# Up projection with the tokens' high and low parts as one 512-column moving operand

## The chip, the cores and the metric

One core of a Trainium2 chip runs the whole layer. The time is that of one execution on the device in microseconds; three runs of the kernel before have a median of 1557.48 us.

## The reference, cut to what matters

One layer of a transformer over 256 tokens of width 2048: an attention block, and then a gated MLP whose up projection is what changes here. All inputs and the output are float32.

```python
z = modulate(rms_norm(x, norm2_g), sh2, sc2)      # 256 x 2048
u = z @ w_up                                      # 256 x 11264 (2 * D_FF, D_FF = 5632)
up = jnp.pad(u, ((0, 0), (1, 1), (0, 0)))
uc = conv_b + sum(conv_w[j] * up[:, j:j + 256] for j in range(3))   # along the tokens
a, b = jnp.split(uc, 2, axis=-1)
x = x + g2 * ((jax.nn.silu(a) * b) @ w_down)
out = rms_norm(x, final_norm_g)
```

## The kernel before

**Three products for one.** A float32 product is made of products of float32r halves. `hi_lo` (line 182) splits a tensor: ScalarE copies it into float32r (`hi`), VectorE subtracts that copy (`lo`). `mm3` then adds three products into a PSUM bank: hi·hi, hi·lo and lo·hi. The first operand is the stationary one (128 x 128), the second the moving one. The tokens' parts in the MLP are `z2h` and `z2l` (tiles sZL and sX in the trace), made by `z2_parts` beside the first products.

**Up projection.** The 11264 columns are 88 tiles of 128. `up_group` (line 1271) takes eight such tiles, and of the last columns of each half four: the weights are stationary, all 256 tokens move, and each tile's result is half of a 512-column PSUM bank. For each of 16 tiles of the contraction (`kt`) a unit of weights (128 x 1024) is multiplied: 8 tiles x 3 products of 256 columns, 24 matmuls. A group fills four of the eight banks; the next group fills the other four while the first is evacuated.

**Weights.** SyncE loads 1 MB (two units) into a ring of four `raw` buffers. Each unit is split into `hi` (ScalarE, CAST) and `lo` (VectorE, TENSOR_TENSOR), of which there are three buffers each: the CAST of a unit waits until TensorE has finished the unit three earlier. `take` keeps two units split ahead of the one in use.

**Evacuation.** `conv` (line 1253) reads the bank: for each tile an ACTIVATE on ScalarE (bias and middle tap), then two SCALAR_TENSOR_TENSOR on VectorE. A group of the first half then gets Silu on ScalarE, one of the second half is multiplied into it on VectorE.

**Order.** TensorE issues in program order. ScalarE and VectorE run in the order in which the scheduler put their instructions. A pacing object lets lanes, the evacuation among them, go a step further when little work is left to VectorE and ScalarE by its estimate. One lane, `rest`, does not belong to the MLP: it forms the gate `g2` out of `w_ada` on VectorE (SCALAR_TENSOR_TENSOR acc<-raw, 128 x 1024) beside the first groups, through the same `raw` ring.

**Down projection.** It follows at once (512-column matmuls, eight banks, the tokens' parts stationary).

Of the kernel before, what the change touches and what calls it, by code (L numbers as in the profile page):

```python
# [10 lines left out]
F32R = mybir.dt.float32r  # L11
# [5 lines left out]
P = 128  # L17
D = 2048
KT = D // P
T = 256  # L20
# [30 lines left out]
class Pace:  # L51
    """Order of emission. TensorE issues in the order emitted; beside the big products run lanes, generators
    that are taken a step further when enough TensorE work lies behind their last step and when VectorE and
    ScalarE have little left to do. A step yields the TensorE time (us) that the next one should stay behind."""
# [51 lines left out]
    def finish(self, *gens):  # L106
        # what is left of these lanes, a step of each in turn
        gens = list(gens)
        self.lanes = [x for x in self.lanes if not any(x[0] is g for g in gens)]
        while gens:  # L110
            gens = [g for g in gens if next(g, None) is not None]
# [7 lines left out]
class Engine:  # L119
    """An engine whose instructions are counted into the pace."""  # L120
# [30 lines left out]
def _build(tc, nc, es, a):  # L151
# [30 lines left out]
    def hi_lo(hi, lo, src):  # L182
        # src = hi + lo exactly: float32r holds the upper half of the significand in hi, the rest in lo
        ACT.copy(hi, src)
        DVE.tensor_sub(lo, src, hi.bitcast(F32))

    def split(src, shape):
        h = units.tile(shape, F32R, tag="hi", name="hi")
        l = units.tile(shape, F32R, tag="lo", name="lo")
        hi_lo(h, l, src)  # L190
        return h, l

    # the weights of the big products, in program order: loaded and split ahead of the products that take them
# [49 lines left out]
    # x and ctx tokens, raw  # L243
# [9 lines left out]
    # conditioning, contraction index k = p * 16 + j  # L253
# [11 lines left out]
    # per-column vectors, turned to one value a partition  # L265
# [25 lines left out]
    def lane_tables():  # L291
        # the other vectors, and the rope tables with the gains of the normalised heads folded in
        r = slot("X0", [P, 4, P])
        POOL.memset(r, 0.0)
        nc.sync.dma_start(r[0:88, 0, :], a["conv_b"][0].rearrange("(r c) -> r c", c=P))
        nc.sync.dma_start(r[96:100, 0, :], a["mla_kv_norm_g"][0].rearrange("(r c) -> r c", c=P))
        nc.sync.dma_start(r[100:106, 0, :], a["mla_q_norm_g"][0].rearrange("(r c) -> r c", c=P))
        for j in range(3):
            nc.sync.dma_start(r[0:88, 1 + j, :], a["conv_w"][0, j].rearrange("(r c) -> r c", c=P))
        nc.sync.dma_start(tabB, a["ropeB"].rearrange("w (t p) d -> p w t d", p=P))  # L300
        nc.sync.dma_start(tabA, a["ropeA"].rearrange("w (t p) d -> p w t d", p=P))
        nc.sync.dma_start(gqk[:, 0, :], a["gqa_q_norm_g"].partition_broadcast(P)[:, 0, :])
        nc.sync.dma_start(gqk[:, 1, :], a["gqa_k_norm_g"].partition_broadcast(P)[:, 0, :])
        yield 25.0
        turn_vectors(1, 4, flat(r))
        yield 0.0
        for w in range(2):
            g = gqk[:, w, :]
            gv = g.rearrange("p (x h q) -> p x h q", x=2, h=2)
            for t in range(2):  # L310
                DVE.tensor_mul(tabG[:, w, 0, t, :], tabB[:, 0, t, :], g)
                o = tabG[:, w, 1, t, :].rearrange("p (x h q) -> p x h q", x=2, h=2)
                s = tabB[:, 1, t, :].rearrange("p (x h q) -> p x h q", x=2, h=2)
                for h in range(2):
                    DVE.tensor_mul(o[:, :, h, :], s[:, :, h, :], gv[:, :, 1 - h, :])
                yield 0.0

# [63 lines left out]
    def gemv_chunk(ci):  # L381
        # first shift and scale of both conditionings, the columns that part ci of the contraction needs
# [111 lines left out]
    # how many of its loads it may take: a result's slot has to be free when it comes to it  # L494
# [24 lines left out]
    def group_T(ps, w, mov, first, last):  # L519
        wh, wl = w  # L520
        mh, ml = mov
        for n in range(wh.shape[1] // P):
            mm3(ps[n // 2][:, (n % 2) * T:(n % 2 + 1) * T], wh[:, n * P:(n + 1) * P], wl[:, n * P:(n + 1) * P],
                mh, ml, first and n % 2 == 0, last)

# [87 lines left out]
    # the same blocks' weights  # L613
    def rows2(w, nk, c0, cn, kt0=0):
        # one k tile a unit, two a load
        for k0, kn in halves(nk):
            r = load(w[(kt0 + k0) * P:(kt0 + k0 + kn) * P, c0:c0 + cn].rearrange("(k p) c -> p k c", p=P), [P, kn, cn])
            for k in range(kn):
                yield split(r[:, k, :], [P, cn])

    def weights():
# [30 lines left out]
        for g in range(6):  # L652
            for half in range(2):
                yield from rows2(a["w_up"][0], KT, half * FF + g * 1024, min(8, FT - 8 * g) * P)
# [5 lines left out]

    stream = weights()
# [57 lines left out]
    def rope(dst, src, cc, ssn, heads, q, tA, tB):  # L719
        # dst = src * cc + swap(src) * ssn, heads of 4 * q columns  # L720
# [89 lines left out]
    def attn_head(passes, scale, v, oh, ol, ptag):  # L810
        # one head: scores of both query tiles, softmax over all keys, P V
# [147 lines left out]
    # branch B's attention beside the last part of the input projection  # L959
# [258 lines left out]
    z2h = [slot(f"ZL{i}", [P, 8, T], F32R) for i in range(2)]  # L1218
    z2l = [slot(f"X{2 + i}", [P, 8, T], F32R) for i in range(2)]

    def z2_parts():
        for n in range(4):
# [5 lines left out]
            for j in range(0, 4, 2):  # L1228
# [4 lines left out]
                for k in range(2):  # L1233
# [3 lines left out]
                    hv, lv = z2h[kt // 8][:, kt % 8, :], z2l[kt // 8][:, kt % 8, :]  # L1237
# [15 lines left out]
    def conv(dst, ps, col, turns):  # L1253
        # two tiles of columns, their steps in turn or one after the other
# [16 lines left out]
    def up_group(g, half, zgen=None):  # L1271
        nt = min(8, FT - 8 * g)
        if half == 0:
            hid.append(slot(hslots[g], [P, nt, T]))
        hs = hid[g]
        c0 = half * FF + g * 1024
        ps = [bank() for _ in range(nt // 2)]
        for kt in range(KT):
            w = take()
            if zgen is not None and kt % 2 == 0:  # L1280
                next(zgen, None)
            group_T(ps, w, (z2h[kt // 8][:, kt % 8, :], z2l[kt // 8][:, kt % 8, :]), kt == 0, kt == KT - 1)
            yield

        def end():
            for n2 in range(nt // 2):
                hv = flat(hs[:, 2 * n2:2 * n2 + 2, :])
                d = hv if half == 0 else scratch([P, 512])
                conv(d, ps[n2], c0 // P + 2 * n2, (g, half) == (5, 1))
# [24 lines left out]
    for g in range(6):  # L1314
        for half in range(2):
            run(up_group(g, half, zgen if g + half == 0 else None))
# [6 lines left out]
    w_d = a["w_down"][0]  # L1323
    ps = [[bank() for _ in range(4)] for _ in range(2)]
# [18 lines left out]
    # the last part bank by bank, so that the end of one runs beside the products of the next  # L1343
# [47 lines left out]
def _rope_tables(rot):  # L1391
    # cos and signed sin of the grid positions, laid out as (axis, half, frequency) columns
# [29 lines left out]
```

## Time and profile before

| | |
|---|---|
| three runs | 1556.18, 1557.48, 1559.08 us |
| profiled execution, span | 1556.9 us |
| TensorE busy | 1514.9 us, 97% |
| VectorE busy | 1079.2 us, 69% |
| ScalarE busy | 747.3 us, 48% |
| up projection, first product to last | about 791 to 1307 us |
| down projection | from about 1307 us |

Times in the trace count from the span's start. An engine's busy time is what its instructions took; overlapping ones count once. PEld is TensorE's weight load, which runs beside the products. DMA share is the mean busy share of the core's 16 DMA engines. The profiled execution's span lies 0.6 us under the median of the runs.

### The profile page before, as it was taken

How to read it: one execution, taken by the hardware profiler on the slowest of the kernel's cores; microseconds unless marked ns; L12 is line 12 of the kernel's file. 1: busy time of each engine (PE TensorE's matmuls, PEld its weight loads, DVE VectorE, ACT ScalarE, POOL GpSimd, SP SyncE). 2: the span in 40 equal slices, each digit the busy share in tenths (PEclk: the TensorE clock that was granted, in tenths of full speed). 3: DMA queues.
4: the chain of work that ended last, by engine and by line, in shares of the span. 5: the costliest groups of instructions: out<-in, count | busy, mean ns of one | idle time of the engine just before them, and what ended most of it. 6: DMA issues, size and time to landing. Idle time of an engine off the chain costs nothing.

```text
span 1556.9 us, 25677 instructions
## 1 busy us (share of the span) xinstructions
PE 1514.9 (97%) x10641; PEld 1387.7 (89%) x10641; DVE 1079.2 (69%) x1489; ACT 747.3 (48%) x1081; POOL 14.3 (1%) x23
## 2 busy tenths in 40 slices
PE   6999999999999999999989999999999999999997
PEld 5777888899998988997879999999999999888886
DVE  3457686798778888697878787656546566555556
ACT  4634242355775446543346445454444545444454
POOL 0000000010000000000000000000000000000000
PEclk9999999999999999999989999999999999999999
DMA  9778788755346885478967877555555447555552
GB/s 359 240 252 321 276 323 286 259 180 190 109 143 201 288 279 187 160 265 307 350 217 249 318 278 273 182 182 173 187 190 185 162 141 245 189 192 195 199 197 81
DMA packets 105380, 350.59 MB, mean 225 GB/s; under 512 B 6846, under 2 KB 20392, under 8 KB 98736
## 3 DMA queue, kind: packets, MB, share of 16 engines
q1 hardware_dynamic: 105264, 348.96, 64.8%
q8 instruction: 83, 1.36, 0.3%
q14 instruction: 33, 0.27, 0.1%
HBM read 346.84 MB, written 2.10 MB: 224 GB/s over the span
## 4 chain that ended last, share of the span: by engine, by line
PE 90%; DMA 5%; DVE 3%; ACT 1%; issue 1%; SPq 0%; ACTq 0%; POOLq 0%; POOL 0%; DVEq 0%
PE bank L210 86%; DMA raw<-in_w_ada 2%; PE bank L219 2%; PE bank L398 2%; DMA raw<-in_w_in 1%; DVE lo L140 1%; DVE acc L140 1%; DMA raw<-in_w_out 1%; DVE sK L140 1%; DMA sK<-in_x 0%; DVE sX L140 0%; DVE scratch L140 0%; ACT hi L140 0%; ACT scratch L140 0%; DVE sG L140 0%
## 5 line engine op out<-in xcount | busy, mean ns | idle before, releaser
L140 DVE TENSOR_TENSOR lo<-raw,hi 128x1024 fp32r<-128x1024 f32 (+3 forms) x479 | 551.6, 1154 | 336.5 <-ACT hi L140 333.3
L140 ACT CAST hi<-raw 128x1024 fp32r<-128x1024 f32 (+3 forms) x479 | 474.6, 993 | 624.3 <-PE bank L210 512.9
L210 PE MATMUL bank<-sZL,hi 128*128 128x256 f32 (+1 forms) x3168 | 740.9, 285 | 2.5 <-ACT hi L140 2.5
L210 PE MATMUL bank<-sZL,lo 128*128 128x256 f32 x2352 | 667.5, 284 | 0.6 <-DVE lo L140 0.6
L210 PEld LDWEIGHTS bank<-sZL,hi 128*128 128x128 f32 (+1 forms) x3168 | 551.4, 192 | 14.5 <-issue 7.5
L210 PEld LDWEIGHTS bank<-sZL,lo 128*128 128x128 f32 x2352 | 452.2, 192 | 1.1 <-DVE lo L140 1.1
L210 PE MATMUL bank<-sX,hi 128*128 128x256 f32 x1536 | 435.6, 284 | 0.5 <-DVE sX L140 0.5
L210 PEld LDWEIGHTS bank<-sX,hi 128*128 128x128 f32 x1536 | 295.8, 193 | 1.3 <-DVE sX L140 0.8
L210 PE MATMUL bank<-hi,sZC 128*128 128x512 f32 (+1 forms) x816 | 261.1, 383 | 0.0
L210 PEld LDWEIGHTS bank<-hi,sZC 128*128 128x128 f32 x816 | 152.5, 188 | 30.0 <-issue 0.3
L140 DVE SCALAR_TENSOR_TENSOR acc<-raw,cs,acc 128x1024 f32<-128x1024 f32 x120 | 153.6, 1280 | 14.2 <-DMA raw<-in_w_ada 13.2
L210 PE MATMUL bank<-lo,sZC 128*128 128x512 f32 (+1 forms) x344 | 131.4, 382 | 0.0
L210 PEld LDWEIGHTS bank<-lo,sZC 128*128 128x128 f32 x344 | 64.7, 188 | 12.8 <-DVE lo L140 0.3
L140 DVE TENSOR_TENSOR sK<-bank,sK 128x512 f32<-128x512 f32 (+1 forms) x92 | 59.9, 685 | 10.1 <-PE bank L210 8.8
L210 PE MATMUL bank<-hi,sZL 128*128 128x512 f32 x192 | 63.3, 392 | 0.0
L210 PE MATMUL bank<-lo,sX 128*128 128x512 f32 x128 | 50.1, 391 | 1.9 <-DVE lo L140 1.9
L210 PE MATMUL bank<-sZC,hi 128*128 128x256 f32 x256 | 50.4, 284 | 1.4 <-DVE sZC L140 1.4
L210 PE MATMUL bank<-hi,sX 128*128 128x512 f32 x128 | 50.4, 394 | 0.1
L140 DVE TENSOR_TENSOR sG<-bank,sG 128x512 f32<-128x512 f32 x64 | 41.9, 683 | 5.9 <-PE bank L210 5.8
L210 PEld LDWEIGHTS bank<-hi,sZL 128*128 128x128 f32 x192 | 36.1, 188 | 9.4 <-issue 1.5
L398 PE MATMUL bank<-raw,cs 128*32 128x512 f32 (+2 forms) x320 | 37.7, 514 | 5.1 <-DMA raw<-in_w_ada 4.9
L210 PEld LDWEIGHTS bank<-sZC,hi 128*128 128x128 f32 x256 | 39.0, 184 | 2.5 <-DVE sZC L140 1.6
(195 smaller groups left out, 1266.7 us busy)
## 6 DMA issues: line engine op xcount, KB each, us to landing
raw<-in_w_ada SPq DMA_DIRECT2D x82, 1024.0 KB, 5.7
raw<-in_w_up SPq DMA_DIRECT2D x80, 1024.0 KB, 5.1
raw<-in_w_down SPq DMA_DIRECT2D x44, 1024.0 KB, 4.9
raw<-in_w_in SPq DMA_DIRECT2D x37, 1024.0 KB, 7.6
raw<-in_w_out SPq DMA_DIRECT2D x16, 1024.0 KB, 8.3
raw<-in_w_ada SPq DMA_DIRECT2D x16, 768.0 KB, 6.1
raw<-in_w_br_b SPq DMA_DIRECT2D x8, 1024.0 KB
raw<-in_w_br_a SPq DMA_DIRECT2D x8, 1024.0 KB, 6.7
```

Of the source, the lines that this page charges most:

```text
L140: return f(*args, **kw)
L210: PE.matmul(out, lhsT, rhs, start=start, stop=stop, skip_group_check=True)
L219: PE.transpose(out, src, ident[:n, :n])
L398: PE.matmul(ps[32 * g:32 * g + 32, :cols], cs[:, j0 + jj, :], w[:, jj, :], start=j0 + j == 0, stop=j0 + j == 14, skip_group_check=True)
```

## The change

The first group (8 tiles, `up_first`) keeps the old products, since the tokens' parts are only then being made. The other 80 tiles go in 20 parts of four (`up_part`). Tile and bank are now one to one: a single matmul multiplies the weights' hi with hi and lo of the tokens side by side (2 x 256 columns), so that hi·hi lies in the first half of the bank and hi·lo in the second, and a second matmul of 256 columns adds lo·hi to the second half. At the end `halves_sum` copies the first half to SBUF and adds the second to it; `conv` reads that sum. A unit of weights is now 2 contraction tiles x 512 columns, and a load 4 x 512 columns: as many bytes as before, in rows of 2 KB instead of 4 KB.

```diff
-    z2h = [slot(f"ZL{i}", [P, 8, T], F32R) for i in range(2)]
-    z2l = [slot(f"X{2 + i}", [P, 8, T], F32R) for i in range(2)]
+    z2 = [slot(x, [P, 2, 4, T], F32R) for x in ("ZL0", "ZL1", "X2", "X3")]
...
+    def group_W(ps, wh, wl, mov, first, last):
+        for n, p in enumerate(ps):
+            c = slice(n * P, (n + 1) * P)
+            mm(p.rearrange("p (s t) -> p s t", s=2), wh[:, c], mov, first, False)
+            mm(p[:, T:2 * T], wl[:, c], mov[:, 0, :], False, last)
+
+    def halves_sum(ps):
+        u = scratch([P, 512])
+        for i in range(2):
+            ACT.copy(u[:, i * T:(i + 1) * T], ps[i][:, 0:T])
+        for i in range(2):
+            d = u[:, i * T:(i + 1) * T]
+            DVE.tensor_add(d, ps[i][:, T:2 * T], d)
+        return u
...
+    def rows4(w, nk, c0):
+        for k0 in range(0, nk, 4):
+            r = load(w[k0 * P:(k0 + 4) * P, c0:c0 + 512].rearrange("(k p) c -> p k c", p=P), [P, 4, 512])
+            for u in range(2):
+                yield split(r[:, 2 * u:2 * u + 2, :], [P, 2, 512])
...
-        for g in range(6):
-            for half in range(2):
-                yield from rows2(a["w_up"][0], KT, half * FF + g * 1024, min(8, FT - 8 * g) * P)
+        yield from rows2(a["w_up"][0], KT, 0, 1024)
+        for c0 in up_cols[1:]:
+            yield from rows4(a["w_up"][0], KT, c0)
...
+    def up_part(g, half, sub):
+        hs = hid[g]
+        c0 = (half * FF + g * 1024 + sub * 512) // P
+        ps = [bank() for _ in range(4)]
+        for k2 in range(0, KT, 2):
+            wh, wl = take()
+            for k in range(2):
+                kt = k2 + k
+                group_W(ps, wh[:, k, :], wl[:, k, :], z2[kt // 4][:, :, kt % 4, :], kt == 0, kt == KT - 1)
+                yield
+
+        def end():
+            us = []
+            for n2 in range(2):
+                us.append(halves_sum(ps[2 * n2:2 * n2 + 2]))
+                yield 0.0
+            for n2 in range(2):
+                hv = flat(hs[:, 4 * sub + 2 * n2:4 * sub + 2 * n2 + 2, :])
+                d = hv if half == 0 else scratch([P, 512])
+                conv(d, us[n2], c0 + 2 * n2, (g, half) == (5, 1))
...
-    ps = [[bank() for _ in range(4)] for _ in range(2)]
+    ps = [[None] * 4 for _ in range(2)]
+    for n2 in range(0, 4, 2):
+        for t in range(2):
+            for n in range(n2, n2 + 2):
+                ps[t][n] = bank()
```

On TensorE, inside a group of the up projection, two tiles before (sZL is the tokens' hi, sX their lo; hi and lo without a prefix are the weights'):

```order
L210 MATMUL bank<-sZL_8144,hi 128x256
L210 MATMUL bank<-sX_8146,hi 128x256
L210 MATMUL bank<-sZL_8144,lo 128x256
L210 MATMUL bank<-sZL_8144,hi 128x256
L210 MATMUL bank<-sX_8146,hi 128x256
L210 MATMUL bank<-sZL_8144,lo 128x256
```

and the end of the first group and the first three tiles of a part now (one tile, sZL_8144, holds hi and lo):

```order
L210 MATMUL bank<-sX_8147,hi 128x256 x2
L210 MATMUL bank<-sX_8147,lo 128x256
L210 MATMUL bank<-sZL_8144,hi 128x512
L210 MATMUL bank<-sZL_8144,lo 128x256
L210 MATMUL bank<-sZL_8144,hi 128x512
L210 MATMUL bank<-sZL_8144,lo 128x256
L210 MATMUL bank<-sZL_8144,hi 128x512
```

Three matmuls for a tile have become two, with as many columns in all.

On VectorE, where a group of the first half ends late in the up projection (sX is the group's result), before:

```order
L140 TENSOR_TENSOR lo<-raw,hi 128x1024 x11
L140 SCALAR_TENSOR_TENSOR sX_12348<-bank,vec,sX_12348 128x255 x4
L140 TENSOR_TENSOR lo<-raw,hi 128x1024
L140 SCALAR_TENSOR_TENSOR sX_12348<-bank,vec,sX_12348 128x255 x4
L140 TENSOR_TENSOR lo<-raw,hi 128x1024
```

and where a part with the same columns ends now (scratch is the sum's buffer):

```order
L140 TENSOR_TENSOR lo<-raw,hi 128x1024 x5
L140 TENSOR_TENSOR scratch<-bank,scratch 128x256 x3
L140 TENSOR_TENSOR lo<-raw,hi 128x1024
L140 TENSOR_TENSOR scratch<-bank,scratch 128x256
L140 SCALAR_TENSOR_TENSOR sX_11626<-scratch,vec,sX_11626 128x255 x8
L140 TENSOR_TENSOR lo<-raw,hi 128x1024 x7
```

The splits were interleaved with four steps of the convolution at a time; now four adds and eight such steps stand round a single split.

On ScalarE at the same place now:

```order
L140 COPY scratch<-bank 128x256 x3
L140 CAST hi<-raw 128x1024
L140 COPY scratch<-bank 128x256
L140 ACTIVATE sX_11626<-scratch,vec 128x256 x4
L140 CAST hi<-raw 128x1024
L140 ACTIVATE sX_11626<-sX_11626 128x512
L140 CAST hi<-raw 128x1024
```

The four COPY are new; the second CAST stands behind four ACTIVATE that each wait for an add.

## Rows read from the trace of the kernel before

**Rows 1.** The page: span, TensorE, and the chain that ended last.

```profile
span 1556.9 us, 25677 instructions
...
PE 1514.9 (97%) x10641; PEld 1387.7 (89%) x10641; DVE 1079.2 (69%) x1489; ACT 747.3 (48%) x1081; POOL 14.3 (1%) x23
...
PE 90%; DMA 5%; DVE 3%; ACT 1%; issue 1%; SPq 0%; ACTq 0%; POOLq 0%; POOL 0%; DVEq 0%
```

**Rows 2.** Stretches: PE, PEld, DVE, ACT, POOL busy (records); clock, DMA share, GB/s.

```profile
890.50:936.60 46.10, 46.10 (x387) 46.10 (x386) 40.09 (x48) 21.42 (x27) 0.00 (x0) 1.00 0.80 292
1000.00:1290.00 290.00, 290.00 (x2419) 290.00 (x2419) 172.14 (x227) 138.43 (x176) 0.00 (x0) 1.00 0.53 174
1265.00:1300.00 35.00, 35.00 (x294) 35.00 (x293) 24.86 (x44) 18.99 (x33) 0.00 (x0) 1.00 0.66 197
1320.00:1500.00 180.00, 180.00 (x796) 149.10 (x795) 94.72 (x100) 79.97 (x100) 0.00 (x0) 1.00 0.57 194
```

**Rows 3.** Groups by form, 830 to 1290 us: busy, mean ns | idle before.

```profile
L210 PE MATMUL bank<-sZL,hi 128*128 128x256 f32 x1268 | 359.7, 284 | 0.0
...
L140 DVE TENSOR_TENSOR lo<-raw,hi 128x1024 fp32r<-128x1024 f32 x147 | 179.9, 1224 | 138.8 <-ACT hi L140 137.0
L140 ACT CAST hi<-raw 128x1024 fp32r<-128x1024 f32 x146 | 152.9, 1047 | 209.4 <-PE bank L210 203.2 <-issue 4.5 <-ACT scratch L140 0.9
L140 DVE SCALAR_TENSOR_TENSOR scratch<-bank,vec,scratch 128x255 f32<-128x255 f32 x80 | 35.0, 477 | 0.4
L140 DVE SCALAR_TENSOR_TENSOR acc<-raw,cs,acc 128x1024 f32<-128x1024 f32 x26 | 33.3, 1281 | 3.8 <-DMA raw<-in_w_ada 3.6
...
L140 ACT ACTIVATE scratch<-bank,vec 128x256 f32<-128x256 f32 x40 | 21.5, 564 | 7.3 <-DVE scratch L140 5.7 <-PE bank L210 1.3
...
L140 DVE TENSOR_TENSOR sG<-sG,scratch 128x512 f32<-128x512 f32 x16 | 11.0, 688 | 0.1
```

**Rows 4.** TensorE timeline where lengths mix (attention's value products): start us, us.

```profile
561.53 0.28 PE L210 MATMUL bank<-hi,sK 128*128 128x256 f32 x1
561.65 0.63 PE L210 MATMUL bank<-sK,hi 128*128 128x512 f32 x2
...
562.81 0.39 PE L210 MATMUL bank<-sK,lo 128*128 128x512 f32 x1
563.04 0.28 PE L210 MATMUL bank<-hi,sK 128*128 128x256 f32 x1
563.15 0.28 PE L210 MATMUL bank<-lo,sK 128*128 128x256 f32 x1
```

**Rows 5.** Groups by form, whole run: the nearest to the new operations.

```profile
L140 ACT ACTIVATE sZC<-sX,md 128x256 fp32r<-128x256 f32 x16 | 8.7, 591 | 1.1 <-DVE sX L140 1.1
...
L140 DVE TENSOR_TENSOR sX<-bank,sZL 128x256 fp32r<-128x256 f32 x8 | 3.4, 419 | 0.9 <-ACT sZL L140 0.9
...
L140 ACT COPY sY<-bank 128x256 f32<-128x256 f32 x8 | 2.9, 365 | 1.5 <-PE bank L210 1.5
```

**Rows 6.** VectorE timeline at a group's end: start us, us.

```profile
983.78 1.65 DVE L140 SCALAR_TENSOR_TENSOR scratch<-bank,vec,scratch 128x255 f32<-128x255 f32 x4
985.52 1.23 DVE L140 TENSOR_TENSOR lo<-raw,hi 128x1024 fp32r<-128x1024 f32 x1
986.66 1.65 DVE L140 SCALAR_TENSOR_TENSOR scratch<-bank,vec,scratch 128x255 f32<-128x255 f32 x4
```

**Rows 7.** ScalarE timeline inside a group, with what ended its wait.

```profile
1021.88 1.05 ACT L140 CAST hi<-raw 128x1024 fp32r<-128x1024 f32 x1 [1.83 <-PE bank L210]
```

**Rows 8.** VectorE timeline, the same unit's lo.

```profile
1022.95 1.23 DVE L140 TENSOR_TENSOR lo<-raw,hi 128x1024 fp32r<-128x1024 f32 x1 [1.66 <-ACT hi L140]
```

**Rows 9.** TensorE timeline, first units of the down projection.

```profile
1311.47 0.74 PE L210 MATMUL bank<-hi,sZC 128*128 128x512 f32 x2
...
1313.12 0.40 PE L210 MATMUL bank<-hi,sZC 128*128 128x512 f32 x1
```

**Rows 10.** Waits: ScalarE's for the loads of the up weights, 770 to 1300 us.

```profile
ACT hi L140 <- DMA raw<-in_w_up: 3.1, 1, 3.1
```

More of the change, by code (lines that the diff above doesn't have):

```diff
@@ L659, in weights @@
                 yield (hx, *split(r[:, u * 1024:(u + 1) * 1024], [P, 1024]))
+    up_parts = [(0, 0, None)]
+    for g in range(6):
+        for half in range(2):
+            for sub in range(min(8, FT - 8 * g) // 4):
+                if g + half > 0:
+                    up_parts.append((g, half, sub))
+    up_cols = [0] + [half * FF + g * 1024 + sub * 512 for g, half, sub in up_parts[1:]]
     stream = weights()
@@ L1236, in z2_parts @@
                     pv = ps[:, k * T:(k + 1) * T]
-                    hv, lv = z2h[kt // 8][:, kt % 8, :], z2l[kt // 8][:, kt % 8, :]
+                    hv, lv = z2[kt // 4][:, 0, kt % 4, :], z2[kt // 4][:, 1, kt % 4, :]
                     ACT.activation(hv, pv, AF.Identity, bias=s2col[:, kt:kt + 1], scale=a2col[:, kt:kt + 1])
@@ L1269, in h_split, with up_first @@
         return hx
[L1271 to L1277, printed above, removed]
+    def up_first(zgen):
+        ps = [bank() for _ in range(4)]
         for kt in range(KT):
             w = take()
-            if zgen is not None and kt % 2 == 0:
+            if kt % 2 == 0:
                 next(zgen, None)
-            group_T(ps, w, (z2h[kt // 8][:, kt % 8, :], z2l[kt // 8][:, kt % 8, :]), kt == 0, kt == KT - 1)
+            group_T(ps, w, (z2[kt // 4][:, 0, kt % 4, :], z2[kt // 4][:, 1, kt % 4, :]), kt == 0, kt == KT - 1)
             yield
         def end():
-            for n2 in range(nt // 2):
-                hv = flat(hs[:, 2 * n2:2 * n2 + 2, :])
+            for n2 in range(4):
+                hv = flat(hid[0][:, 2 * n2:2 * n2 + 2, :])
+                conv(hv, ps[n2], 2 * n2, False)
+                yield 0.0
+                ACT.activation(hv, hv, AF.Silu)
+                yield 0.0
+        evacs["up"] = pace.add(end(), limit=LIM_EVAC, prio=0)
+    def up_part(g, half, sub):
+        hs = hid[g]
+        c0 = (half * FF + g * 1024 + sub * 512) // P
+        ps = [bank() for _ in range(4)]
+        for k2 in range(0, KT, 2):
[8 more added lines that the diff above has]
+                us.append(halves_sum(ps[2 * n2:2 * n2 + 2]))
+                yield 0.0
+            for n2 in range(2):
+                hv = flat(hs[:, 4 * sub + 2 * n2:4 * sub + 2 * n2 + 2, :])
                 d = hv if half == 0 else scratch([P, 512])
-                conv(d, ps[n2], c0 // P + 2 * n2, (g, half) == (5, 1))
+                conv(d, us[n2], c0 + 2 * n2, (g, half) == (5, 1))
                 yield 0.0
@@ L1313, in _build @@
     pace.add(rest, after=20.0, limit=REST_LIM_U, dma=REST_DMA, prio=9)
-    for g in range(6):
-        for half in range(2):
-            run(up_group(g, half, zgen if g + half == 0 else None))
+    for g, half, sub in up_parts:
+        if half == 0 and not sub:
+            hid.append(slot(hslots[g], [P, min(8, FT - 8 * g), T]))
+        run(up_first(zgen) if sub is None else up_part(g, half, sub))
     finish(evacs["up"])
```

## The prediction

> **What bounds the kernel now.** I read the page first: TensorE is busy for 97% of the span, and the chain that ended last is 90% TensorE [rows 1]. So the question is what TensorE does in the up projection and whether anything makes it wait there. The groups of 830 to 1290 us give each of the three kinds of products no idle time before it [rows 3], and the stretch of 1000 to 1290 us has TensorE and its weight load busy throughout at the full granted clock of 1.00, the 2.4 GHz level, while VectorE is busy for 59% and ScalarE for 48% [rows 2]. TensorE's stream alone sets the time here; the rest has room. Busy time of overlapping matmuls says nothing of the price of one, so I take start-to-start times from counts: 2419 records less some three that reach over the edges in 290 us are 0.120 us for a matmul of 256 columns, and 796 less two in 180 us of the down projection are 0.227 us for one of 512 [rows 2]. At 2.4 GHz the columns alone would take 0.1067 and 0.2133 us: both lengths carry the same 13 to 14 ns on top. That is what the change works on.
>
> **What it removes.** For one tile and one contraction tile, three matmuls of 256 columns (0.360 us) become one of 512 and one of 256 (0.347 us). Where the lengths mix today, 256 columns are followed by the next matmul after 0.12 us and 512 columns after 0.23 us [rows 4], so I add the two prices. Saved: 13 ns, 80 tiles x 16 times, 1280 x 0.013 = **16.6 us**. The first group, 8 tiles, keeps its price. The clock is not at stake: it is 1.00 in all these stretches [rows 2], and TensorE remains without pauses if the rest of this working holds.
>
> Here a rule speaks against the size of it. The page "TensorE: Matmul & The Clock Gate" of the Trainium skill (section "Wait — 56ns, not 53.3ns?") gives a warm matmul a fixed cost of about 2.5 ns over its columns. By that the saving would be 1280 x 2.5 ns = 3.2 us, an estimate from that page. The trace does not agree: 13.3 ns over 256 columns and 13.7 over 512.
>
> **What it adds.** Each of the 80 tiles gets a COPY on ScalarE and an add on VectorE. The nearest rows are a COPY of 128 x 256 from a bank, 365 ns, and an add of 128 x 256 with a bank as one input, 419 ns [rows 5]. The convolution now reads SBUF: its ACTIVATE costs 591 ns [rows 5] for 564 [rows 3]; its SCALAR_TENSOR_TENSOR I leave at 477. In all 33.5 us for VectorE and 80 x (0.365 + 0.027) = 31 us for ScalarE, none of it on the path if TensorE covers it. A part lasts 64 x 0.347 = 22.2 us on TensorE. VectorE has in it eight splits, four adds and eight steps, 9.8 + 1.7 + 3.8 = 15.3 us, in the second half of the columns two products of 0.69 more, 16.7: 69 to 75%. ScalarE has 8 x 1.047 + 4 x 0.365 + 4 x 0.591 = 12.2 us and at times Silu. So the cover is there on average. Without it all 33.5 us would go on the path.
>
> The average is not the danger; the order at a part's end is. Today a split's CAST starts when TensorE frees the buffer at 1021.88, lo is ready at 1024.18 [rows 7, 8], and TensorE first wants it two units later, 2 x 24 x 0.120 us plus two matmuls, at about 1027.8. The reserve is 3.6 us. At the end of a part of the first half, counted from its last matmul: three COPY lie almost wholly before it, since the banks finish 0.35 us apart; the first CAST ends at 1.2, the fourth COPY at 1.5, its four ACTIVATE at 3.4 to 3.9, the next CAST at 4.4 to 5.0 us. VectorE: the lo of the first CAST until 2.4, the fourth add until 2.9, then eight steps. Alone one takes 0.48 us, in a row four take 1.65 [rows 6], about 0.39 each, so they end at 6.0 to 6.7 and the lo of the second CAST at 7.2 to 7.9. TensorE wants this unit after three units of 2.78 us, its lo one matmul later, at 8.55. The reserve shrinks to 0.7 to 1.3 us, but stays above nothing. Cost there: 0.
>
> Two places have less cover. In the first six parts the gate's steps run as well: the program order puts 24 of 1.28 us [rows 3] there, four in a part, which makes 20.4 to 21.8 us of 22.2 by single durations, and some tenth less by the pace of instructions in a row (a lo of 1.23 us is followed after 1.14 [rows 6]). That is 85 to 98%. Today the fullest group has VectorE busy for 40.09 of 46.1 us, 87%, and its 387 records are still 0.120 us apart [rows 2]. The bounds are 0 and what two gate steps at the wrong place would take beyond a reserve of 1.3 us at each of six ends, 6 x (2.56 - 1.3) = 7.6 us. The row of 87% without any loss is the nearer; I take 0.5.
>
> The other is the step to the down projection. It loses 0.3 us today: six matmuls from 1311.47 to 1313.12, 1.65 us for 1.36 [rows 9]. An add now stands among the steps before the third unit's lo. Its banks come free early, since an add and not the convolution ends their use. Bounds 0 and 1 us; I take 0.2, half of the add.
>
> The loads keep their bytes, but in rows of 2 KB. Where the last groups load such rows today, 197 GB/s take a DMA share of 0.66, against 174 at 0.53 with 4 KB [rows 2]: a tenth dearer. At 1 MB in 5.55 us that is a share of about 0.63, beside the gate's loads some 0.9. ScalarE waited once, for 3.1 us, for a load of these weights [rows 10], and TensorE for none. I count 0; the upper bound belongs to the six parts above.
>
> **Sum:** -16.6 + 0.5 + 0.2 = -15.9 us. The profiled span of 1556.9 becomes 1541.0; it lies 0.6 us under the median of the runs, so I predict 1541.6.
>
> **The rivals.** *Late splits in the six full parts.* The mechanism is right, and the gate's steps or loads eat up to 7.6 us and the step to the down projection 1: a gain of 8 to 13 us, 1545 to 1550. For it speak the 98%; against it the 87% without loss.
>
> *Late splits at every part's end, and slower.* The COPY, add, ACTIVATE and step chain is handed between two engines that work in order, and the second split stands behind all of it. If that lo ends 1.5 to 2.2 us later than I sum, it is 0.83 us late, and at 20 ends that is 16.6 us, the whole gain: this is the point from which it decides. At 1.5 us late it would be 30, and the kernel would take 1571. Against it: CAST ends at 1022.93 and lo starts at 1022.95 [rows 7, 8], so a hand-over costs next to nothing.
>
> *The change does not do what it says.* The moving operand has two runs of 256 columns, 4 KB apart. If each run is paid like a matmul, 2 x 0.120, a tile costs 0.360 as before, and 1557.5 + 0.7 = 1558 remains. The trace has no 512 columns in two runs; but the 256 columns of [rows 4] are two runs of 128 and cost the 0.12 of a single run.
>
> *Most of the 13 ns goes with the columns.* If only 2.5 ns belonged to an instruction and the other 11 to each 256 columns, the tile would cost 0.3575, the saving be 3.2 us and the time 1555.0. Against it: 512 columns would then have 24 ns on top and have 13.7; with the weight load busy for only 149.10 of 180 us [rows 2] it isn't that load either. (That is the outcome by the Trainium skill's rule named above.)
>
> **How the numbers follow.** The forecast, a gain of 13 to 18 us, has a chance of 0.77; late splits in six parts 0.13; late everywhere 0.05; two runs paid singly 0.03; the columns' 13 ns 0.02. About 0.2%, 3.1 us, is what this measurement tells from no change. Faster by more: 0.77 + 0.13 = 0.90; the same: 0.03 + 0.02 = 0.05; slower: 0.05. The range goes from 1537, the full 16.6 us with nothing given back and the runs' own spread of 1.5 us on top, with two more for the prices' last digit, to 1550, the first rival's end; it leaves out the other rivals' 0.10.
>
> **What would show it.** In the profile after: between the first group and the down projection, matmuls start 0.227 and 0.120 us apart in turn, and a part lasts 22.2 us; the down projection begins near 1291 instead of 1307. VectorE's and ScalarE's busy time grow by some 30 us each while TensorE's idle time in the stage remains under 2 us. A copy of about 0.37 and an add of about 0.42 us confirm the prices. I am wrong if the 512-column matmul with two runs takes more than 0.23 us, or if TensorE waits for lo at each part's end, above all at the fourth unit of a part.

## The result and the profile after

The changed kernel takes 1549.63 us (1548.86 to 1550.32) beside 1558.24 us (1556.18 to 1559.08) for the kernel before: a ratio of 0.9949 with an interval of 0.9935 to 0.9963. The gain is 8.6 us by the medians and 7.9 by the ratio (5.8 to 10.1 by its interval), about half of the forecast 15.9. The time lies inside the range, 0.4 us from its upper end.

From the page after (span, busy time, chain; compare [rows 1]):

```profile
span 1548.5 us, 23200 instructions
...
PE 1506.7 (97%) x9361; PEld 1320.4 (85%) x9361; DVE 1102.8 (71%) x1553; ACT 769.6 (50%) x1145; POOL 14.2 (1%) x23
...
PE 87%; DVE 6%; DMA 5%; ACT 1%; issue 1%; SPq 0%; ACTq 0%; POOLq 0%; POOL 0%; DVEq 0%
```

1280 matmuls are gone, and TensorE still fills 97% of the span. The stretches after (columns as in [rows 2]):

```profile
830.00:1000.00 170.00, 170.00 (x986) 147.59 (x985) 145.05 (x193) 94.79 (x133) 0.00 (x0) 1.00 0.77 267
1000.00:1280.00 280.00, 280.00 (x1587) 242.92 (x1586) 184.49 (x264) 151.53 (x216) 0.00 (x0) 1.00 0.57 188
```

A pair is one 512-column product and the 256-column product behind it. TensorE has no pause from 1000 to 1280 us and the granted clock is 1.00, the 2.4 GHz level, so the count gives the price: 1587 records less two at the edges, halved, are 792.5 pairs in 280 us, **0.3533 us a pair**, where the forecast had 0.347 and three matmuls had taken 0.360 [rows 2]. 1280 pairs save 1280 x 0.0067 = 8.5 us: the whole measured gain. The start times agree: from the first product of these 80 tiles to the first down product it is 455.7 us after (842.31 to 1298.02) and 464.2 before (842.69 to 1306.91).

The groups by form of 830 to 1290 us show what was added (columns as in [rows 3]):

```profile
L140 DVE TENSOR_TENSOR lo<-raw,hi 128x1024 fp32r<-128x1024 f32 x162 | 197.5, 1222 | 118.3 <-ACT hi L140 117.8
...
L140 DVE SCALAR_TENSOR_TENSOR scratch<-scratch,vec 128x255 f32<-128x255 f32 x80 | 34.1, 477 | 0.0
...
L140 DVE TENSOR_TENSOR scratch<-bank,scratch 128x256 f32<-128x256 f32 x76 | 29.3, 422 | 1.8 <-ACT scratch L140 1.8
L140 ACT COPY scratch<-bank 128x256 f32<-128x256 f32 x76 | 27.5, 374 | 15.0 <-PE bank L210 15.0
L140 ACT ACTIVATE scratch<-scratch,vec 128x256 f32<-128x256 f32 x40 | 20.8, 599 | 0.0
```

Each is within 9 ns of its forecast price. VectorE still stands idle for 117.8 us before the splits, so it has room. The missing gain must be in the products themselves. TensorE's timeline after, in the middle of a part (start us, us):

```profile
1074.71 0.40 PE L210 MATMUL bank<-sZL,hi 128*128 128x512 f32 x1
1074.94 0.28 PE L210 MATMUL bank<-sZL,lo 128*128 128x256 f32 x1
1075.06 0.40 PE L210 MATMUL bank<-sZL,hi 128*128 128x512 f32 x1
1075.30 0.28 PE L210 MATMUL bank<-sZL,lo 128*128 128x256 f32 x1
1075.42 0.40 PE L210 MATMUL bank<-sZL,hi 128*128 128x512 f32 x1
1075.65 0.28 PE L210 MATMUL bank<-sZL,lo 128*128 128x256 f32 x1
1075.77 0.40 PE L210 MATMUL bank<-sZL,hi 128*128 128x512 f32 x1
```

From one 512 to the next it is 0.35, 0.36, 0.35 us, and so on: a period of three pairs (to the nanosecond 0.350, 0.361, 0.349), kept through all 20 parts. The mean 512 takes 0.2367 and the mean 256 takes 0.1167 us, where pure streams have 0.227 and 0.120.

### The profile page after: what moved, and what is told of

Same layout as the page of the kernel before. It is cut to its first block, busy times and chain, and to the rows that moved or that the text cites. A ratio compares the mean times of both kernels' runs of the same rounds, so it can differ in the third digit from the quotient of the medians.

```text
span 1548.5 us, 23200 instructions
## 1 busy us (share of the span) xinstructions
PE 1506.7 (97%) x9361; PEld 1320.4 (85%) x9361; DVE 1102.8 (71%) x1553; ACT 769.6 (50%) x1145; POOL 14.2 (1%) x23
## 4 chain that ended last, share of the span: by engine, by line
PE 87%; DVE 6%; DMA 5%; ACT 1%; issue 1%; SPq 0%; ACTq 0%; POOLq 0%; POOL 0%; DVEq 0%
PE bank L210 84%; DMA raw<-in_w_ada 3%; PE bank L398 2%; PE bank L219 2%; DVE acc L140 1%; DVE lo L140 1%; DMA raw<-in_w_in 1%; DVE sK L140 1%; DVE scratch L140 1%; DMA raw<-in_w_out 1%; ACT scratch L140 1%; DMA sK<-in_x 0%; DVE sX L140 0%; DVE st L140 0%; ACT hi L140 0%
## 5 line engine op out<-in xcount | busy, mean ns | idle before, releaser
L140 DVE TENSOR_TENSOR lo<-raw,hi 128x1024 fp32r<-128x1024 f32 (+2 forms) x463 | 548.3, 1188 | 301.2 <-ACT hi L140 299.5
L140 ACT CAST hi<-raw 128x1024 fp32r<-128x1024 f32 (+2 forms) x463 | 472.0, 1022 | 581.1 <-PE bank L210 463.8
L210 PE MATMUL bank<-sZL,hi 128*128 128x256 f32 (+2 forms) x2528 | 591.7, 315 | 3.0 <-ACT hi L140 2.5
L210 PE MATMUL bank<-sZL,lo 128*128 128x256 f32 (+1 forms) x1648 | 466.4, 283 | 0.6 <-DVE lo L140 0.6
L210 PEld LDWEIGHTS bank<-sZL,hi 128*128 128x128 f32 (+1 forms) x2528 | 421.0, 191 | 44.7 <-issue 7.5
L210 PEld LDWEIGHTS bank<-sZL,lo 128*128 128x128 f32 (+1 forms) x1648 | 314.6, 191 | 1.1 <-DVE lo L140 1.1
L210 PE MATMUL bank<-sX,hi 128*128 128x512 f32 (+1 forms) x896 | 287.5, 367 | 0.0
L210 PE MATMUL bank<-sX,lo 128*128 128x256 f32 x704 | 197.8, 281 | 0.0
L210 PEld LDWEIGHTS bank<-sX,hi 128*128 128x128 f32 x896 | 164.7, 189 | 30.4 <-issue 0.5
L140 DVE SCALAR_TENSOR_TENSOR acc<-raw,cs,acc 128x1024 f32<-128x1024 f32 x120 | 153.6, 1280 | 16.3 <-DMA raw<-in_w_ada 15.4
L210 PEld LDWEIGHTS bank<-sX,lo 128*128 128x128 f32 x704 | 133.2, 189 | 0.5 <-issue 0.5
```

The lines of the kernel that those rows point to most:

```text
L140: return f(*args, **kw)
L210: PE.matmul(out, lhsT, rhs, start=start, stop=stop, skip_group_check=True)
```

## The experiments

Each kernel ran beside the kernel before on one chip, but not all on the same one; ratios are to that run of the kernel before. Pairs are read from the start times of 512-column products in each kernel's own trace. "Parts" runs, by the same start times, from the first product of the 80 tiles that the change touches to the first down product. It is the sharper measure: what lies ahead of the up projection, and no edit touches, varies by 8 us between the profiled executions (the first up product starts at 786 to 794 us), and the medians carry some of that.

| kernel | median us | ratio (95%) | pair us | parts us |
|---|---|---|---|---|
| before | 1558.24 | | 0.360 (three) | 464.2 |
| after | 1549.63 | 0.9949 (0.9935 to 0.9963) | 0.3533 | 455.7 |
| one_run | 1549.64 | 0.9948 (0.9931 to 0.9965) | 0.3533 | 455.7 |
| first_half | 1549.13 | 0.9944 (0.9927 to 0.9962) | 0.3533 | 455.7 |
| batch4 | 1544.87 | 0.9917 (0.9898 to 0.9937) | 0.3508 | 452.5 |
| batch8 | 1543.58 | 0.9910 (0.9891 to 0.9929) | 0.3492 | 450.9 |
| batch16 | 1542.89 | 0.9913 (0.9900 to 0.9926) | 0.3479 | 449.0 |
| three256 | 1558.23 | 1.0008 (0.9999 to 1.0017) | 0.360 (three) | 464.2 |
| extra_dve | 1542.64 | 0.9915 (0.9899 to 0.9932) | 0.3533, then 0.3467 | 449.5 |
| sums_moved | 1543.43 | 0.9910 (0.9894 to 0.9925) | 0.3533, then 0.3467 | 448.3 |
| extra_quiet | 1550.06 | 0.9954 (0.9941 to 0.9967) | 0.3533 | 455.7 |
| hiccup_once | 1539.81 | 0.9889 (0.9874 to 0.9904) | 0.3467 | 447.2 |
| hiccup_all | 1548.15 | 0.9939 (0.9925 to 0.9953) | 0.3467 and 0.3533 by turns | 454.1 |
| hiccup_later | 1548.84 | 0.9945 (0.9932 to 0.9958) | 0.3533 | 455.7 |

### What makes the pair dearer than the sum of its prices?

Four explanations stood against each other: the change of length from product to product costs time; the moving operand's two runs cost it; the 256-column product waits for columns that were written just before; or the `lo` weights come too late.

**one_run** stores hi and lo of a contraction tile side by side, so that the 512 columns are one run.

```diff
-    z2 = [slot(x, [P, 2, 4, T], F32R) for x in ("ZL0", "ZL1", "X2", "X3")]
+    z2 = [slot(x, [P, 4, 2, T], F32R) for x in ("ZL0", "ZL1", "X2", "X3")]
...
```

> The only edit: hi and lo of the tokens lie side by side, so that the 512 columns of the moving operand are one run and not two. A pair (512 and 256 columns) takes 0.3533 us in the changed kernel, where the pure streams of before give 0.347. Theory A (change of length costs: in the trace of before, the first five 512-column matmuls after 256-column ones take 0.233, 0.236, 0.228, 0.233, 0.231 instead of 0.227 us): pair stays 0.353, time 1549.6. Rival B (the second run of the moving operand costs some 6 ns): pair 0.347, 1280 x 6.3 ns = 8 us less, 1541.6. Rival C (the narrow product adds to the half that the wide one has just written, and waits for it): pair stays 0.353, 1549.6.

The pair stays at 0.3533 us, the parts at 455.7 and the time at 1549.64. The second run costs nothing.

**first_half** adds lo·hi to the other half of the bank.

```diff
-            mm(p[:, T:2 * T], wl[:, c], mov[:, 0, :], False, last)
+            mm(p[:, 0:T], wl[:, c], mov[:, 0, :], False, last)
```

> The only edit: the narrow product (weights' lo) is added to the first half of the bank, not to the second, which the wide product wrote last. The sum over the halves is the same. Theory A (change of length): pair stays 0.353 us, time 1549.6. Rival B (two runs): the same. Rival C (the narrow product waits for columns just written): pair 0.347, 8 us less, 1541.6.

0.3533 again: which half was written last does not matter.

**batch4** issues the four 512s of a contraction tile, then its four 256s.

```diff
-        for n, p in enumerate(ps):
-            c = slice(n * P, (n + 1) * P)
+        cs_ = [slice(n * P, (n + 1) * P) for n in range(4)]
+        for p, c in zip(ps, cs_):
             mm(p.rearrange("p (s t) -> p s t", s=2), wh[:, c], mov, first, False)
+        for p, c in zip(ps, cs_):
             mm(p[:, T:2 * T], wl[:, c], mov[:, 0, :], False, last)
```

> The same products in another order: for each contraction tile the four wide products, then the four narrow ones. Theory A: a run of four wide ones has 22 ns on top by the trace of before and the narrow ones give 6 back, 16 ns in four pairs, 4 ns a pair instead of 6.3: pair 0.351, 3 us less, 1546.7. Rival B (two runs): pair stays 0.353, 1549.6. Rival C (columns just written; now three other banks lie between): pair 0.347, 1541.6.

**batch8** does it for a unit of weights, two contraction tiles.

```diff
...
-                group_W(ps, wh[:, k, :], wl[:, k, :], z2[kt // 4][:, :, kt % 4, :], kt == 0, kt == KT - 1)
+                wide(ps, wh[:, k, :], z2[kt // 4][:, :, kt % 4, :], kt == 0)
                 yield
+            for k in range(2):
+                kt = k2 + k
+                narrow(ps, wl[:, k, :], z2[kt // 4][:, :, kt % 4, :], kt == KT - 1)
```

> The same products in another order: for each unit of weights (two contraction tiles) the eight wide products, then the eight narrow ones. Theory A: a run of eight has 26 ns on top and 6 back, 20 ns in eight pairs, 2.5 ns a pair: pair 0.3495, 5 us less, 1544.7. Rival B: pair stays 0.353, 1549.6. Rival C: pair 0.347, 1541.6.

The pair falls to 0.3508 and 0.3492 us, and against the change as made the parts are 3.2 and 4.8 us shorter (5 and 6 us by the medians). Above 0.3467 that is 4 x 4.1 = 16 ns for one round of four and four, 8 x 2.5 = 20 ns for eight and eight. So a run's first products carry the extra: in the traces with mixed lengths the first five 512s behind 256s take 0.233, 0.236, 0.228, 0.233 and 0.231 us, 26 ns more than five pure ones, and the first 256 behind 512s gives 6 back. But batch8 and batch4 also ask for `lo` later, which the fourth explanation would like as well.

**batch16** separates these: one unit goes wide then narrow and the next narrow then wide, so that runs are 16 long while every second unit wants its `lo` first.

```diff
...
+            for step in ("wn" if k2 % 4 == 0 else "nw"):
+                for k in range(2):
+                    kt = k2 + k
+                    if step == "w":
+                        wide(ps, wh[:, k, :], z2[kt // 4][:, :, kt % 4, :], kt == 0)
+                    else:
+                        narrow(ps, wl[:, k, :], z2[kt // 4][:, :, kt % 4, :], False)
```

> As batch8, but units alternate: wide then narrow, in the next unit narrow then wide, so that runs of sixteen of a length meet. By theory A (a change of length costs, about 20 ns for a run of wide ones and the narrow ones after it) one change falls on sixteen pairs: 1.2 ns a pair, pair 0.3483 us against 0.3492 in batch8 and 0.3533 in the changed kernel; 1280 x 5.0 ns = 6.4 us less than the changed kernel, 1543.2 beside 1549.6. Rival D (what helped in batch4 and batch8 was that a unit's lo is wanted later, not the runs): here lo is wanted first in every other unit, so the time goes back to 1549 or more.

The stretch of 1000 to 1280 us of batch16:

```profile
1000.00:1280.00 280.00, 280.00 (x1611) 247.42 (x1610) 187.36 (x269) 151.60 (x218) 0.00 (x0) 1.00 0.56 187
```

2 x 280 / 1609 = 0.3480 us there, 0.3479 over whole rounds: 16 x 1.2 = 19 ns a round, with `lo` wanted earlier. Late `lo` is out; in these three orders the cost goes with the number of changes of length. That a change of length need not cost anything is shown further down.

**three256** takes the joint operand back and keeps the rest of the change: parts of four, halves, copies, adds, loads.

```diff
-            mm(p.rearrange("p (s t) -> p s t", s=2), wh[:, c], mov, first, False)
+            mm(p[:, 0:T], wh[:, c], mov[:, 0, :], first, False)
+            mm(p[:, T:2 * T], wh[:, c], mov[:, 1, :], False, False)
```

> The joint moving operand alone is undone: three products of 256 columns for a tile, as before, all of them 0.120 us apart; the layout of a bank for each tile, the loads in rows of 2 KB, the copies, the adds and the order remain. What the change adds is then seen without what it saves. Prediction's sum: 0.7 us, so 1558.3 beside 1557.6 for the kernel before. Rival (the added copies, adds and loads cost several us, and ate the half of the saving): 1563 to 1566.

1.0008: all that the change adds costs -0.2 to 2.6 us by the interval, and nothing in the parts by the trace, 464.2 us as before. The forecast had 0.7, of it 0.5 there.

**extra_dve** was to show how much room VectorE has: one more 128 x 256 instruction behind each add.

```diff
             DVE.tensor_add(d, ps[i][:, T:2 * T], d)
+            DVE.tensor_scalar(out=d, in0=d, scalar1=1.0, scalar2=None, op0=ALU.mult)
```

> The changed kernel with one more VectorE instruction of 128 x 256 behind each add (times 1.0), 80 of about 0.4 us, 33 us more on VectorE in the chain at each part's end. If the chain's reserve is as the prediction summed it (0.7 to 1.3 us for the second split, four more instructions take 1.4 to 1.7 us), TensorE is 0.1 to 1 us late at each end of a part of the first half, ten of them: 1 to 10 us more, 1551 to 1560. If the reserve is larger than summed: 1549.6.

This fell outside every expectation: with more work the kernel was *faster* than the change as made, by 7 us in the medians and 6.2 in the parts. Its trace has 0.3533 us a pair in the first two parts and most of the third, and then 0.3467 to the end, the sum of the two pure prices. TensorE's timeline of extra_dve at the turn, and the only product that waited for `lo`:

```profile
904.20 0.40 PE L210 MATMUL bank<-sX,hi 128*128 128x512 f32 x1
904.44 0.28 PE L210 MATMUL bank<-sX,lo 128*128 128x256 f32 x1
904.56 0.40 PE L210 MATMUL bank<-sX,hi 128*128 128x512 f32 x1
904.80 0.28 PE L210 MATMUL bank<-sX,lo 128*128 128x256 f32 x1
904.91 1.88 PE L210 MATMUL bank<-acc,ones 128*128 128x512 f32 x4
906.23 0.80 PE L210 MATMUL bank<-sX,hi 128*128 128x512 f32 x1
906.87 0.28 PE L210 MATMUL bank<-sX,lo 128*128 128x256 f32 x1
906.98 0.39 PE L210 MATMUL bank<-sX,hi 128*128 128x512 f32 x1
...
978.60 0.38 PE L210 MATMUL bank<-sZL,lo 128*128 128x256 f32 x1 [0.86 <-DVE lo L140]
```

So the late `lo` that the run was made for came once, in the first pair behind the sixth part, and cost 1.1 us; the pairs cost 0.3467 before and behind it.

Between the dear pairs (0.3533) and the cheap ones (0.3467) stand the sums of the gate (acc, ones), four 512-column products of the lane `rest`. They stand in the stream after too, at 900.26 us, and there the pairs went on as before. But the planner (the pacing object) had counted the extra work, and so had put these sums behind 180 pairs instead of 164. Numbered from 0, the next pair is 180 instead of 164; divided by three, 164 leaves 2 and 180 leaves 0: another place in the period of three. That made a new theory: strict alternation has **two steady states**, and a break in the stream decides by its place in the period which one follows.

### Is it the break, or the work on VectorE?

**sums_moved** is the change as made with the first gate sums four pairs later, behind 168 pairs, and nothing else moved (the sums are a lane's step; it now waits longer).

```diff
-                    yield 3.0
+                    yield 12.0 if vname == "g2" and sec == 0 else 3.0
```

> The changed kernel, with the first of the two pairs of gate sums (TensorE, 128x512 over acc and ones) issued one contraction tile later, behind pair 168 of the up stage's 1280 in place of 164; nothing else moves. In the changed kernel the pairs cost 0.3533 us all through, in a period of three; in the run with the extra VectorE instruction they fell to 0.3467 exactly behind these sums, which stood there behind pair 180. 164 leaves the rest 2 when divided by three, 168 and 180 leave 0. Theory E (the pairs have two steady states, and a break in the stream of products decides which one follows by where it falls in the period of three): 0.3467 from pair 168 on, so 1112 pairs by 6.7 ns, 7.4 us less than the changed kernel, 1542.2 us, and a mean pair of 0.3475. Rival F (the extra VectorE work itself, by what it reads and writes, makes the products faster): nothing changes, 0.3533 and 1549.6.

TensorE's timeline of sums_moved at these sums, and its stretch of 1000 to 1280 us:

```profile
902.59 0.40 PE L210 MATMUL bank<-sX,hi 128*128 128x512 f32 x1
902.83 0.28 PE L210 MATMUL bank<-sX,lo 128*128 128x256 f32 x1
902.94 1.88 PE L210 MATMUL bank<-acc,ones 128*128 128x512 f32 x4
904.25 0.80 PE L210 MATMUL bank<-sX,hi 128*128 128x512 f32 x1
904.89 0.28 PE L210 MATMUL bank<-sX,lo 128*128 128x256 f32 x1
905.01 0.39 PE L210 MATMUL bank<-sX,hi 128*128 128x512 f32 x1
905.24 0.28 PE L210 MATMUL bank<-sX,lo 128*128 128x256 f32 x1
905.36 0.39 PE L210 MATMUL bank<-sX,hi 128*128 128x512 f32 x1
```

```profile
1000.00:1280.00 280.00, 280.00 (x1618) 246.87 (x1617) 187.71 (x270) 154.86 (x219) 0.00 (x0) 1.00 0.55 189
```

0.3533 us a pair before these sums; behind them 0.347, 0.346, 0.347 to the nanosecond (2 x 280 / 1616 = 0.3465 us in that stretch), and it holds through the second sums to the end. 1543.43 us for an expected 1542.2.

**extra_quiet** has the extra VectorE work without the planner's knowledge, so that TensorE's program is that of the change.

```diff
             DVE.tensor_add(d, ps[i][:, T:2 * T], d)
+            nc.vector.tensor_scalar(out=d, in0=d, scalar1=1.0, scalar2=None, op0=ALU.mult)
```

> The extra VectorE instruction (a 128x256 multiply by one behind each addition of halves) again, but not counted by the planner, so that TensorE's program is that of the changed kernel, with the gate sums behind pairs 164 and 380. Theory E (the place of a break decides between the two states): the pairs stay at 0.3533, 1549.6 us, unless VectorE's work makes TensorE wait for a part's weights and so breaks the stream at another place; each such wait of about 1 us would stand in the trace, and the fall to 0.3467 would come right behind one. Rival F (the VectorE work itself makes the products faster): 0.3467 from the second or third part on with no break before it, 1542.

Its stretch of 1000 to 1280 us:

```profile
1000.00:1280.00 280.00, 280.00 (x1587) 242.91 (x1586) 192.79 (x311) 152.31 (x215) 0.00 (x0) 1.00 0.55 188
```

0.3533 in all 20 parts, parts of 455.7 us and a time of 1550.06 us; no product waits. The work itself does nothing for or against; what the planner moved because of it did.

### Is a pause needed, and does the place decide?

**hiccup_once** changes two neighbours at one place: in the second contraction tile of the first new part the products go wide, wide, narrow, narrow, and from there on alternate as before.

```diff
...
+        if swap:
+            for f, n in ((wide, 0), (wide, 1), (narrow, 0), (narrow, 1)):
+                f(n)
+        for n in range(2 if swap else 0, 4):
+            wide(n)
+            narrow(n)
...
+                        kt == 1 and (g, half, sub) == (0, 1, 0))
```

> The changed kernel with two products exchanged at one place: in the second contraction tile of the first new part the first four products go wide, wide, narrow, narrow; the other 1278 pairs alternate as before. Theory E: this too breaks the alternation, with no wait. If the place suits, the pairs cost 0.3467 from there on, up to 1280 by 6.7 ns, 8.5 us less than the changed kernel, 1541.1; if it does not, 0.3533 and 1549.6. A lasting change of the pair's price from an exchange of two products speaks for E either way round; rival G (only a stop of TensorE, such as the 0.64 us at the gate sums, can change the state) says 0.3533 and 1549.6.

TensorE's timeline of hiccup_once at the exchange, and then at the place shown above of the change as made, with the stretch of 1000 to 1280 us:

```profile
840.92 0.40 PE L210 MATMUL bank<-sZL,hi 128*128 128x512 f32 x1
841.15 0.28 PE L210 MATMUL bank<-sZL,lo 128*128 128x256 f32 x1
841.27 0.64 PE L210 MATMUL bank<-sZL,hi 128*128 128x512 f32 x2
841.74 0.40 PE L210 MATMUL bank<-sZL,lo 128*128 128x256 f32 x2
841.98 0.40 PE L210 MATMUL bank<-sZL,hi 128*128 128x512 f32 x1
...
1074.91 0.39 PE L210 MATMUL bank<-sZL,hi 128*128 128x512 f32 x1
1075.14 0.28 PE L210 MATMUL bank<-sZL,lo 128*128 128x256 f32 x1
1075.26 0.39 PE L210 MATMUL bank<-sZL,hi 128*128 128x512 f32 x1
1075.49 0.28 PE L210 MATMUL bank<-sZL,lo 128*128 128x256 f32 x1
1075.61 0.39 PE L210 MATMUL bank<-sZL,hi 128*128 128x512 f32 x1
1075.84 0.28 PE L210 MATMUL bank<-sZL,lo 128*128 128x256 f32 x1
1075.95 0.39 PE L210 MATMUL bank<-sZL,hi 128*128 128x512 f32 x1
```

```profile
1000.00:1280.00 280.00, 280.00 (x1617) 246.90 (x1616) 186.72 (x267) 153.72 (x216) 0.00 (x0) 1.00 0.56 192
```

2 x 280 / 1615 = 0.3467 us; that price holds from the exchange to the end of the stage, 446 us and some 1270 pairs, through both gate sums. To the nanosecond the pairs take 0.350 and 0.343 by turns up to the second sums, and 0.346 to 0.347 each behind them, as in sums_moved: the cheap price has two patterns. One exchange of two products is worth 8.5 us by the parts (455.7 to 447.2) and 9.8 by the medians: 1539.81 us, the lowest median of all, and faster than the change as made by intervals that don't meet (0.9874 to 0.9904 against 0.9935 to 0.9963).

**hiccup_all** makes the exchange in each of the 20 parts (`kt == 1`).

> The same exchange of two products in the second contraction tile of each of the 20 new parts. A part has 64 pairs, which leaves 1 when divided by three, so the exchange falls at a different place of the period from part to part as long as the period lasts. Theory E: within the first two or three parts one of them falls right, and then 0.3467 holds as far as no later exchange undoes it: 1541 to 1544 us. Rival G (an exchange changes nothing that lasts): 0.3533 and 1549.6, less 20 times the few ns of a run of two.

Half right. The theory holds, my count of it did not: an exchange can also lead back. The first leads to 0.3467, the second, out of the cheap state, to 0.3533; the third does nothing; then the gate sums lead to the cheap state again, the fourth exchange leaves it so and the fifth ends it. The sixth to eighth parts repeat this with the second sums. From the eighth exchange on the pairs are at 0.3533 for good, since each exchange starts the period afresh and the next one, 64 pairs on, always falls at the same place, one that changes nothing. TensorE's timeline of hiccup_all at the second exchange, where the step from 0.35 and 0.34 back to 0.35 and 0.36 begins:

```profile
861.05 0.39 PE L210 MATMUL bank<-sZL,hi 128*128 128x512 f32 x1
861.28 0.27 PE L210 MATMUL bank<-sZL,lo 128*128 128x256 f32 x1
861.40 0.62 PE L210 MATMUL bank<-sZL,hi 128*128 128x512 f32 x2
861.86 0.40 PE L210 MATMUL bank<-sZL,lo 128*128 128x256 f32 x2
862.09 0.40 PE L210 MATMUL bank<-sZL,hi 128*128 128x512 f32 x1
```

Between the first exchange and this one the pairs take 0.347 us in the mean; from 862.09 on they take 0.351, 0.361, 0.349.

**hiccup_later** is hiccup_once one contraction tile later, behind pair 8 in place of 4 (`kt == 2`).

> The exchange of hiccup_once (two products, one place, first new part) one contraction tile later: behind pair 8 in place of pair 4. In the period of three of the changed kernel the long pair (0.361 us) is every pair whose number, from 0, leaves 1; the exchange that led to 0.3467 began at pair 4, a long one, and the later exchanges of hiccup_all that changed nothing all began at the pair right behind a long one, as pair 8 is. Theory E (the place in the period decides): the pairs stay at 0.3533 in all 20 parts and the time at 1549.6 us, so that the same edit brings nothing. Rival H (any first exchange in the stream leads to the cheap state, and place does not matter): 0.3467, 1540.

Its stretch of 1000 to 1280 us:

```profile
1000.00:1280.00 280.00, 280.00 (x1587) 242.91 (x1586) 183.06 (x260) 150.82 (x214) 0.00 (x0) 1.00 0.54 187
```

0.3533 us in all 20 parts, parts of 455.7 us, and 1548.84 us: the same edit at another place is worth nothing.

The breaks that fell into the dear state, from the start times of all these traces. The place is that of the pair that comes next, counted so that the long pair (0.361 us) is 1, the one behind it 2 and the third 0; where an earlier break has shifted the period, it is counted anew:

| break | place | cases | what followed |
|---|---|---|---|
| gate sums | 0 | sums_moved, first; extra_dve, first; hiccup_all, both | 0.3467 |
| gate sums | 1 | hiccup_later, first | 0.3533 |
| gate sums | 2 | after, one_run, first_half, extra_quiet, both; hiccup_later, second | 0.3533 |
| exchange | 1 | hiccup_once; hiccup_all, first | 0.3467 |
| exchange | 2 | hiccup_later; hiccup_all, third, sixth, ninth to twentieth | 0.3533 |

No exchange fell at place 0. In the cheap state the gate sums (four cases) and the wait of extra_dve left the price as it was; of five exchanges of hiccup_all in it, the three that met pairs of 0.350 and 0.343 by turns led to 0.3533, and the two that met even pairs of 0.347 did not.

## Why the prediction was right and wrong

**The bound** was read rightly: TensorE's stream sets the stage's time, before and after, at a clock of 1.00.

**What it removes: right mechanism, a term of the wrong size.** The step that failed is "so I add the two prices". 0.227 and 0.120 us are the prices in streams of one length; the forecast's 0.347 us a pair was not what the change runs at, but 0.3533, and so 16.6 us became 8.5. The sum is not impossible: hiccup_once reaches 0.3467 and parts 17.0 us shorter than before. The change as made enters the dear state behind the first group, and neither of its two breaks leads out of it. The doubt was in sight: in [rows 4] five 512s behind a 256 go from 561.65 to 562.81, 1.16 us for 5 x 0.227 = 1.135 (three of them stand where lines are left out). I read these rows in hundredths and as single prices; as a sum they show some 0.025 us, 26 ns by the start times to the nanosecond. What the two states would do could not be read from the kernel before, which never alternates the lengths.

**What it adds** was sized rightly: 374 ns for 365, 422 for 419, 599 for 591, 477 for 477, and all of it beside TensorE. three256 has the whole cost at -0.2 to 2.6 us for the forecast 0.7, and none of it in the parts. VectorE's and ScalarE's busy time grew by 24 and 22 us, not by some 30; the durations of their instructions, each counted in full, grew by 31 and 30, and the rest is overlap of neighbours.

**Late splits** did not come. Apart from the gate sums and the step to the down projection no product after is late. The six fuller parts cost nothing; I had put 0.5 there. In the last 14 parts the fourth unit's lo is, as summed, the tightest: it is ready 1.4 to 1.7 us before its product, where the sum left 0.7 to 1.3, and 1.0 to 1.7 in extra_quiet. **The step to the down projection** lost more, as forecast; TensorE's timeline after:

```profile
1303.24 0.61 PE L210 MATMUL bank<-hi,sZC 128*128 128x512 f32 x2
1304.17 0.50 PE L210 MATMUL bank<-lo,sZC 128*128 128x512 f32 x1 [0.32 <-DVE lo L140]
1304.51 0.63 PE L210 MATMUL bank<-hi,sZC 128*128 128x512 f32 x2
```

Three products take 1.27 us for 0.68, so 0.6 is lost where 0.3 was [rows 9], 0.3 more for the 0.2 I took. The down projection begins at 1298 us, not near 1291. **The loads** were not a tenth dearer: 188 GB/s at a share of 0.57 is what 174 at 0.53 was [rows 2].

**The rivals.** Two runs paid singly is refuted by one_run. Late splits, in six parts or everywhere, are refuted by the trace. "Most of the 13 ns goes with the columns" gets nothing from the shortfall: in the cheap state a pair has the whole 13 ns less than three products. The page "TensorE: Matmul & The Clock Gate" of the Trainium skill (section "Wait — 56ns, not 53.3ns?") has 2.5 ns as the cost of one warm matmul over its columns; here 1280 products fewer saved 17.0 us, 13.3 ns each, in hiccup_once, so the trace still disagrees. The time came out between that rival's 1555.0 and the forecast, for a reason that neither had. It also lies among the 1545 to 1550 of "Late splits in the six full parts", whose end is the end of the range, though no split was late: that the range holds it is luck.

**What stays open.** What in TensorE holds a state is not shown. In both the same instructions are issued, the weight load's record starts 2 to 5 ns behind the start of the product before it, and no engine is waited for. The same page of the Trainium skill (section "Back-to-back issue gap") says that in such a stream load and matmul together set the spacing; that would allow for two ways to fit together, but no run here tells them apart. Nor is it shown why a 512 behind 256s is dearer in the first place. Nor why the changes of length cost 16 to 20 ns a round in the batches and nothing in the cheap state, where the length changes with every product. Two rows of the table have one or two cases, and it holds for these two lengths only. The states were read in one profiled execution of each kernel, and the medians agree with them: hiccup_all's profiled execution, 1544.22 us, was the shortest of its five, but its parts of 454.1 us are 1.6 us under the change as made, and its median is 1.5 us under.

## What to carry to other kernels

Prices of matmuls taken from streams of one length need not add up when lengths alternate: bound such a pair from both sides, by the pure sum and by the first products behind a change of length. Where lengths do alternate, look at start-to-start times over many pairs in the profile after; if the pair lies above the sum, exchange two neighbours once, near the start, try it at more than one place, or make the runs longer. An experiment that adds work and makes a kernel faster is worth following: here it was not the work but a break that the plan moved by 16 pairs.

## What the runs showed of the hardware that was not expected

- A stream that strictly alternates 512 and 256 columns has two steady prices at the same granted clock of 1.00, 0.3533 and 0.3467 us a pair, each of which held for some 900 pairs without a break (after and hiccup_once, behind the second gate sums). A single exchange of two products can change either into the other, and four foreign products the dear into the cheap, according to the place.
- Five 512-column products behind 256s take 26 ns more than five of a pure stream; the first 256 behind 512s takes 6 ns less. Runs of 4, 8 and 16 give 0.3508, 0.3492 and 0.3479 us a pair.
- A moving operand in two runs of 256 columns costs no more than one run of 512 (0.3533 us a pair both times).
